# Splitting every fourth feature tile of the up projection by DMAs instead of by ScalarE and VectorE

## The chip, the cores and the metric

The kernel runs on one core of a Trainium2 chip. The time is device microseconds of one execution; the kernel before takes 1145.16 us (median of two runs, 1145.02 and 1145.30). The profile is that of a further execution, whose span, from the first to the last instruction, is 1144.0 us.

## The reference

One layer of a hybrid encoder block on x of shape (1, 256, 2048), all in float32:

```python
proj = x @ w_in                      # 2048 -> 5440, split into retention and latent parts
ret_out = silu(gate) * groupnorm(retention(rope(q), rope(k), v))      # 8 heads of 128
mla_out = latent_attention(c_q, c_kv, k_rope)                          # 8 heads of 128
x = layer_norm(alpha * x + concat(ret_out, mla_out) @ w_out)
h = square(relu(x @ w_up)) @ w_down                                    # 2048 -> 8192 -> 2048
x = layer_norm(alpha * x + h)
```

The change touches `x @ w_up` alone: 2048 by 8192 weights, 64 MB.

## The kernel before

Each large product is made of three cheaper ones. Weights and activations are split into a high part, rounded to the type float32r, and a low part, the rest. High by high, low by high and high by low are summed in PSUM; low by low is left out.

The weights come once from DRAM in the order of their use. A *job* is one load of up to 128 x 2048 floats (1 MB) into one of three raw tiles (`NRAW = 3`), issued on SP's queue (L152). A job is worked off in *pieces* of 1024 columns. For each piece ScalarE casts the raw columns into a high tile (L166) and VectorE subtracts the high tile from the raw one into a low tile (L167). High and low tiles come from a pool with five slots each (`NSLOT = 5`).

The order of the work is that of the program's text; there is no scheduler. After each stretch of matmuls the kernel calls `unit()`, which lets side work advance and then emits further pieces, as many as it is asked for, as long as the piece five before the next one is marked as used (`next_piece`, L113). Whenever a piece of job j is emitted, the loads up to job j + 2 are emitted too.

In the up projection (L864 to L877) one job is one feature tile: 128 output features, 16 blocks of 128 rows of the contraction. A tile `ft` has two pieces of eight blocks. For each block, `wstat` (L582) issues two matmuls: the high weights with 512 columns of activations (both parts of 256 tokens, L584), and the low weights with 256 columns (the high part alone, L585). After each piece its slot is marked free and `unit()` is called, so the end of the first piece of tile ft makes room for the second piece of tile ft + 2, and the end of its second piece makes room for the first piece of tile ft + 3. After a tile's second piece `up_evac` adds the two halves of the PSUM bank (ScalarE's copy, L847, and VectorE's add, L848) and squares the positive part (L849). PSUM has eight banks, taken in turn, so several tiles may wait for their evacuation.

Each engine works its instructions off in the order in which they were emitted; the waits between engines, and those for DMAs, are put in where tiles are shared. GpSimd has the rare powers of minus one half for the norms (L250) and a part of the last norm; between the first layer norm and the second it has nothing to do.

Of the kernel before, what the change touches and what calls it, by code (L numbers as in the profile page):

```python
# [8 lines left out]
F32 = mybir.dt.float32  # L9
# [3 lines left out]
ALU = mybir.AluOpType  # L13
# [23 lines left out]


class Cols:
    """Columns held in pieces of 1024."""  # L40

    def __init__(self, pieces):
        self.pieces = pieces
# [4 lines left out]


class Job:  # L50
    """One load and the pieces of work that it feeds."""

    def __init__(self, load, pieces, slotted):
        self.load = load
# [9 lines left out]
def kernel(  # L64
# [19 lines left out]
    nc = tc.nc  # L84
# [4 lines left out]
    slab = ctx.enter_context(tc.tile_pool(name="slab", bufs=3))  # L89
# [4 lines left out]
    work = work_cm.__enter__()  # L94
    psum = ctx.enter_context(tc.tile_pool(name="psum", bufs=4, space=bass.MemoryType.PSUM))

    def acc(name):
        return psum.tile([P, 512], F32, tag="acc", name=name)
# [1 line left out]
    def bank(name):  # L100
        return psum.tile([P, 512], F32, tag="wk", name=name)

# [1 line left out]
    jobs = []  # L104
    holders = []
    state = {"dma": 0, "job": 0, "unit": 0}
# [31 lines left out]
    def raw_tile(job, name):  # L138
        job.raw = wraw.tile([P, 2048], F32, tag="raw", name=name)
        return job.raw  # L140

    def weights(src, n, name, first=False, into=None):
        job = Job(None, [], into is None)
        cuts = [0, 256, 512, 1024, n]

        def load():
            raw = raw_tile(job, f"raw_{name}")
            if first:
                for a, b in zip(cuts, cuts[1:]):
                    nc.sync.dma_start(raw[:, a:b], src[:, a:b])  # L150
            else:
                nc.sync.dma_start(raw[:, :n], src)  # L152

        def piece(i):
            a, m = i * 1024, min(1024, n - i * 1024)
            if into is None:
                hi = wsp.tile([P, 1024], F32R, tag="hi", name=f"hi_{name}_{i}")
                lo = wsp.tile([P, 1024], F32R, tag="lo", name=f"lo_{name}_{i}")
            else:
                hi, lo = into(i)  # L160
            job.hi.append(hi)
            job.lo.append(lo)
            for o, e in ((0, 256), (256, 512), (512, 1024)) if first and i == 0 else ((0, m),):
                c = slice(o, e)
                r = job.raw[:, a + c.start:a + c.stop]
                nc.scalar.copy(hi[:, c], r)  # L166
                nc.vector.tensor_sub(lo[:, c], r, hi[:, c].bitcast(F32))  # L167

        job.load = load
        job.pieces = [lambda i=i: piece(i) for i in range((n + 1023) // 1024)]  # L170
        job.free = [[False] for _ in job.pieces]
        jobs.append(job)
        return job
# [5 lines left out]
        jobs.append(job)  # L179
        return job  # L180

    # side streams advance one stage for each unit of the main stream of products
    side = []

    def unit(pieces=2):
# [5 lines left out]
            if not next_piece(False):  # L191
                break

# [1 line left out]
    xhl = slab.tile([P, KT, 512], F32R, tag="slab", name="xhl")  # L195

    def x_job(k0, n):
        def load(job):
            nc.sync.dma_start(raw_tile(job, f"xraw{k0}")[:, : n * S], x_t[:, k0 * S:(k0 + n) * S])

        def piece():
            v = job.raw[:, : n * S].rearrange("p (k t) -> p k t", k=n)
            nc.vector.tensor_copy(xhl[:, k0:k0 + n, 0:S], v)
            nc.vector.tensor_sub(xhl[:, k0:k0 + n, S:], v, xhl[:, k0:k0 + n, 0:S].bitcast(F32))

        job = other(load, [piece])

# [1 line left out]
    ident = const.tile([P, P], F32, name="ident")  # L209
    mask = const.tile([P, P], F32, name="mask")  # L210
    invf = const.tile([P, 96], F32, name="invf")
# [38 lines left out]
        nc.gpsimd.tensor_tensor(dst, t[:, :n], mhalf[:, :n], op=ALU.pow)  # L250

    def rot(dst1, dst2, raw, cs, sn, n, w):
        """Rotate n pairs of halves, all first halves ahead of all second ones; raw is used up."""
        c = cs.unsqueeze(1).broadcast_to([P, 2 * n, w])
        s = sn.unsqueeze(1).broadcast_to([P, 2 * n, w])
        v = raw.rearrange("p (a w) -> p a w", w=w)
        t = work.tile([P, 512], F32, tag="t2", name="t2")
        t = t[:, 0:2 * n * w].rearrange("p (a w) -> p a w", w=w)
        nc.vector.tensor_mul(t, v, s)
        nc.vector.tensor_mul(v, v, c)  # L260
        nc.vector.tensor_sub(dst1, v[:, 0:n], t[:, n:2 * n])
        nc.vector.tensor_add(dst2, v[:, n:2 * n], t[:, 0:n])

    def xstat(accs, steps, widths, first, last, tb, banks=None):
        """accs[j] += (h + l)[:, kt, tb].T @ (hi + lo)[:, off + ...] for each
        (hl, kt, hi, lo, off) of steps; l.T @ lo lies below float32's last bit."""
        for i, (hl, kt, hi, lo, off) in enumerate(steps):
            h = hl[:, kt, tb * P:(tb + 1) * P]
            l = hl[:, kt, S + tb * P:S + (tb + 1) * P]
            for x_part, w_part, fst, lst in ((h, hi, True, False), (h, lo, False, False), (l, hi, False, True)):  # L270
                a = off
                for j, w in enumerate(widths):
                    if banks is None or j in banks:
                        nc.tensor.matmul(accs[j][:, :w], x_part, w_part[:, a:a + w],  # L274
                                         start=first and fst and i == 0,
                                         stop=last and lst and i == len(steps) - 1)
                    a += w

# [1 line left out]
    x_job(0, 1)  # L280
    j_mla, j_ret, j_out = [], [], []
    for k in range(KT):
# [34 lines left out]
    for half in range(2):  # L317
        row = []
        for i in range(KT // 2):
            kp = (i + H // 2) % (KT // 2)  # L320
            n = i - (KT // 2 - 3)
            row.append(weights(w_out[half, kp], 2048, f"wo{half}{kp}",
                               into=staged_out(n) if half and n >= 0 else None))
        j_out.append(row)
    j_up = [weights(w_up[ft], 2048, f"wu{ft}") for ft in range(64)]
    j_down = []
    norm_rows = {}

# [16 lines left out]
    row_job(2, [])  # L345
    row_job(3, [])

# [1 line left out]
    nc.gpsimd.memset(warm, 0.0)  # L349
    am = [[acc("m0"), acc("m1"), bank("m2")], [acc("m3"), acc("m4"), bank("m5")]]  # L350
    for i in range(8):
        nc.tensor.matmul(am[1][0][:, 0:P], warm, warm, start=True, stop=True)
    MW = (512, 512, 320)
    # regions of one slab: qnT | knT | v | qrT | krT | kz
    ml = slab.tile([P, 8192], F32, tag="slab", name="ml")
    qnT = ml[:, 0:2048].rearrange("p (h t) -> p h t", h=H)
    knT = ml[:, 2048:4096].rearrange("p (h t) -> p h t", h=H)
    vv = ml[:, 4096:6144].rearrange("p (b c) -> p b c", b=2)
    qrT = ml[:, 6144:7168].rearrange("p (g t) -> p g t", g=4)
    krT = ml[:, 7168:7680].rearrange("p (c t) -> p c t", c=2)  # L360
    lat = ml[:, 2048:2048 + 2 * NMLA].rearrange("p (b c) -> p b c", b=2)
    kz = ml[:, 7680:8192].rearrange("p (b c k) -> p b c k", b=2, c=2)
    nc.gpsimd.memset(kz, 0.0)

    for kt in range(KT):
        hi, lo = use(j_mla[kt])
        last = kt == KT - 1
# [61 lines left out]
    side.append(latent_norm())  # L429
    mix = slab.tile([P, KT, 512], F32R, tag="slab", name="mix")  # L430

# [1 line left out]
    def ret_proj(c, attn):  # L433
        ac = [[acc(f"r{c}_{tb}{j}") for j in range(2)] for tb in range(2)]
        for kp in range(KT // 2):
# [100 lines left out]

    ret_proj(0, ret_attn)

# [1 line left out]
    def q_rope(pq):  # L540
        raw = knT.rearrange("p h t -> p (h t)")[:, 0:1024].rearrange("p (b c) -> p b c", b=2)
        rqo = knT.rearrange("p h t -> p (h t)")[:, 1024:2048].rearrange("p (b h a w) -> p b h a w", b=2, h=8, a=2)
# [17 lines left out]
    for g in range(2):  # L560
        hi, lo = use(j_qr[g])
# [7 lines left out]
    for g in range(2):  # L569
        hi, lo = use(j_uv[g])  # L570
# [17 lines left out]
    for h in range(H):  # L588
        hi, lo = use(j_qk[h])
# [5 lines left out]
        free(j_qk[h])  # L595
        unit()

# [1 line left out]
    att = mid.tile([P, 4, 384], F32, tag="mid", name="att")  # L599

    def mla_attn(h):
# [43 lines left out]
    for c in range(1, 4):  # L645
        ret_proj(c, ret_attn)

# [1 line left out]
    xm = mid.tile([P, 5120], F32, tag="mid", name="xm")  # L649
    xt = xm[:, 0:2 * D].rearrange("p (b c) -> p b c", b=2)  # L650
    spare = xm[:, 2 * D:].rearrange("p (b i c) -> p b i c", b=2, i=4)
# [15 lines left out]
    for half in range(2):  # L667
        ao = [[acc(f"o{half}{tb}{j}") for j in range(2)] for tb in range(2)]
        for i in range(KT // 2 - 3 * half):
            if half == 1 and i == 0:  # L670
                assert not side
                work_cm.__exit__(None, None, None)
                work = ctx.enter_context(tc.tile_pool(name="work2", bufs=1))
            steps = out_steps(half, i)
# [14 lines left out]
        rss[tb] = stat.tile([P, 1], F32, tag="lnrs", name="lnrs")  # L689
        rsqrt_eps(rss[tb], mvs[tb][:, 1:2], 1)  # L690

# [1 line left out]
    w_staged = []  # L693
    for i in range(3):
        w_staged += out_steps(1, KT // 2 - 3 + i)
    x1hl = slab.tile([P, KT, 512], F32R, tag="slab", name="x1hl")
    pts = {}

    # K tiles in order; ks is a range of them
    xf = work.tile([P, 2, 4, P], F32, tag="xf", name="xf")  # L700

    def full(k):
# [32 lines left out]
    first_pb = [acc(f"up{ft}") for ft in range(NSPLIT)]  # L735

    def up_half(tb, ks, fts=range(NSPLIT)):
        """The hi part of the first feature tiles' weights for one block of tokens."""
        t = slice(tb * P, (tb + 1) * P)
        for ft in fts:  # L740
            if ft == len(first_pb):
                first_pb.append(acc(f"up{ft}"))
            hi, lo = use(j_up[ft], (ks[-1] + 8) // 8)
            pb = first_pb[ft].rearrange("p (a t) -> p a t", a=2)
            for k in ks:
                nc.tensor.matmul(pb[:, :, t], hi[:, k * P:(k + 1) * P],  # L746
                                 x1hl[:, k].rearrange("p (a t) -> p a t", a=2)[:, :, t],
                                 start=tb == 0 and k == 0, stop=False)
# [45 lines left out]
    for q in range(3):  # L794
        up_half(0, q4[q])
# [42 lines left out]
    for ft in range(NSPLIT):  # L838
        free(j_up[ft])

# [1 line left out]
    rr = [slab.tile([P, 32, S], F32, tag="slab", name=f"rr{i}") for i in range(2)]  # L842

    def up_evac(ft, pb):
# [19 lines left out]
    for ft in range(NSPLIT, 64):  # L864
        hi, lo = use(j_up[ft])
# [10 lines left out]
                r_split(0)  # L876
            unit()  # L877

# [1 line left out]
    ad = [[(acc if j < 2 else bank)(f"d{tb}{j}") for j in range(4)] for tb in range(2)]  # L880
    for kt in range(60):
        hi, lo = use(j_down[kt])
# [5 lines left out]
        if kt % 4 == 1:  # L888
            r_split(kt // 4 + 1)

# [1 line left out]
    w_staged = []  # L892
    for kt in range(60, 64):
        hi, lo = use(j_down[kt])
# [38 lines left out]
    for j in range(4):  # L933
        down_bank(1, j)
        if j < 2:
            c = (0, j * 512, j * 512 + 512)
# [94 lines left out]
```

## Time and profile before

| | |
|---|---|
| time, median of two runs | 1145.16 us |
| span of the profiled execution | 1144.0 us |
| that execution's time outside the span | taken as the difference to the median, 1.2 us |
| up projection, first to last start of its paired matmuls | 435.9 to 783.2 us |
| TensorE busy, share of the span | 99% |
| VectorE, ScalarE, GpSimd | 60%, 44%, 2% |
| moved by DMA | 217.12 MB, mean 190 GB/s |

Rows of groups read: line, engine, operation, result from operands, shape, count, then busy time in us and the mean of one in ns, then the idle time of the engine just ahead of them and what ended it. Rows of the time order begin with the start and the duration in us; a bracket gives the idle time before and what ended it. Rows of stretches give the stretch, its length, the busy time of TensorE, its weight loads, VectorE, ScalarE and GpSimd with the number of instructions, then the granted TensorE clock (1.00 is full), the busy share of the 16 DMA engines and the GB/s that they moved. Rows of DMA issues end with KB each and the median us from issue to landing. Rows of one tile's instructions give minimum, median and maximum duration in ns and the first and last start.

### The profile page before, as it was taken

How to read it: one execution, taken by the hardware profiler on the slowest of the kernel's cores; microseconds unless marked ns; L12 is line 12 of the kernel's file. 1: busy time of each engine (PE TensorE's matmuls, PEld its weight loads, DVE VectorE, ACT ScalarE, POOL GpSimd, SP SyncE). 2: the span in 40 equal slices, each digit the busy share in tenths (PEclk: the TensorE clock that was granted, in tenths of full speed). 3: DMA queues.
4: the chain of work that ended last, by engine and by line, in shares of the span. 5: the costliest groups of instructions: out<-in, count | busy, mean ns of one | idle time of the engine just before them, and what ended most of it. 6: DMA issues, size and time to landing. Idle time of an engine off the chain costs nothing.

```text
span 1144.0 us, 14163 instructions
## 1 busy us (share of the span) xinstructions
PE 1127.5 (99%) x5636; PEld 952.7 (83%) x5636; DVE 687.6 (60%) x919; ACT 506.7 (44%) x653; POOL 18.2 (2%) x23
## 2 busy tenths in 40 slices
PE   8999999999999999999999999999999999999995
PEld 7888888888888889888888888888888888888884
DVE  5776674666656786555555655555656455445567
ACT  4445664545453545444444444444434444344340
POOL 0000000000000000000000000000000000000003
PEclk9999999999999999999999999999999999999998
DMA  7765364444474625555555555555566555555561
GB/s 227 254 210 208 116 222 178 157 148 160 152 294 177 236 103 196 190 188 190 189 188 185 185 184 184 184 185 184 187 223 237 199 184 189 203 197 184 189 252 74
DMA packets 34049, 217.12 MB, mean 190 GB/s; under 512 B 4160, under 2 KB 5312, under 8 KB 10560
## 3 DMA queue, kind: packets, MB, share of 16 engines
q1 hardware_dynamic: 33552, 215.44, 53.2%
q8 instruction: 44, 0.72, 0.2%
q10 hardware_dynamic: 432, 0.79, 0.2%
q14 instruction: 21, 0.17, 0.0%
HBM read 214.12 MB, written 2.10 MB: 189 GB/s over the span
## 4 chain that ended last, share of the span: by engine, by line
PE 95%; DVE 2%; DMA 1%; POOL 1%; ACT 1%; issue 0%; SPq 0%; ACTq 0%; DVEq 0%; POOLq 0%
PE d L274 29%; PE up L584 20%; PE r L274 15%; PE up L585 10%; PE o L274 7%; PE m L274 4%; PE pu L584 2%; DMA raw_mla<-in_w_mla 1%; PE pv L274 1%; PE pu L585 1%; PE pq L274 1%; PE up L746 1%; PE pms L608 0%; PE pms L607 0%; PE up L754 0%
## 5 line engine op out<-in xcount | busy, mean ns | idle before, releaser
L584 PE MATMUL up<-x1hl,hi_wu 128*128 128x512 f32 x984 | 347.7, 399 | 0.0
L585 PE MATMUL up<-x1hl,lo_wu 128*128 128x256 f32 x984 | 276.4, 281 | 0.0
L274 PE MATMUL d<-hi_wd,rhl 128*128 128x512 f32 x992 | 248.4, 389 | 0.0
L167 DVE TENSOR_TENSOR lo_wd<-raw_wd,hi_wd 128x1024 fp32r<-128x1024 f32 x124 | 146.6, 1221 | 158.3 <-ACT hi_wd L166 158.1
L584 PEld LDWEIGHTS up<-x1hl,hi_wu 128*128 128x128 f32 x984 | 184.9, 188 | 46.0
L274 PEld LDWEIGHTS d<-hi_wd,rhl 128*128 128x128 f32 x992 | 186.2, 188 | 38.6
L166 ACT CAST hi_wd<-raw_wd 128x1024 fp32r<-128x1024 f32 x124 | 125.1, 1053 | 191.3 <-PE d L274 182.8
L167 DVE TENSOR_TENSOR lo_wu<-raw_wu,hi_wu 128x1024 fp32r<-128x1024 f32 x128 | 156.4, 1225 | 74.1 <-ACT hi_wu L166 70.0
L585 PEld LDWEIGHTS up<-x1hl,lo_wu 128*128 128x128 f32 x984 | 185.9, 189 | 0.0
L166 ACT CAST hi_wu<-raw_wu 128x1024 fp32r<-128x1024 f32 x128 | 134.1, 1051 | 83.0 <-PE up L584 80.7
L274 PE MATMUL r<-hi_ret,xhl 128*128 128x512 f32 x512 | 147.1, 397 | 0.0
L274 PE MATMUL d<-lo_wd,rhl 128*128 128x512 f32 x496 | 134.5, 389 | 0.0
L274 PEld LDWEIGHTS d<-lo_wd,rhl 128*128 128x128 f32 x496 | 93.1, 188 | 19.3
L274 PEld LDWEIGHTS r<-hi_ret,xhl 128*128 128x128 f32 x512 | 93.9, 188 | 18.3
L167 DVE TENSOR_TENSOR lo_ret<-raw_ret,hi_ret 128x1024 fp32r<-128x1024 f32 x64 | 75.7, 1220 | 23.0 <-ACT hi_ret L166 22.9
L274 PE MATMUL r<-lo_ret,xhl 128*128 128x512 f32 x256 | 79.4, 391 | 0.0
L847 ACT COPY ut<-up 128x256 f32<-128x256 f32 x64 | 23.9, 373 | 118.9 <-PE up L585 116.2
L166 ACT CAST hi_ret<-raw_ret 128x1024 fp32r<-128x1024 f32 x64 | 64.9, 1051 | 14.5 <-PE r L274 11.6
L848 DVE TENSOR_TENSOR ut<-ut,up 128x256 f32<-128x256 f32 x64 | 27.0, 421 | 65.3 <-ACT ut L847 65.3
L274 PE MATMUL o<-hi_wo,mix 128*128 128x512 f32 x208 | 57.1, 392 | 0.0
L274 PEld LDWEIGHTS r<-lo_ret,xhl 128*128 128x128 f32 x256 | 48.0, 188 | 10.4
L274 PE MATMUL m<-hi_mla,xhl 128*128 128x512 f32 (+1 forms) x192 | 46.1, 372 | 0.9 <-ACT hi_mla L166 0.8
(182 smaller groups left out, 980.7 us busy)
## 6 DMA issues: line engine op xcount, KB each, us to landing
raw_wu<-in_w_up SPq DMA_DIRECT2D x64, 1024.0 KB, 4.8
raw_wd<-in_w_down SPq DMA_DIRECT2D x64, 1024.0 KB, 4.8
raw_ret<-in_w_ret SPq DMA_DIRECT2D x32, 1024.0 KB, 4.8
raw_wo<-in_w_out SPq DMA_DIRECT2D x16, 1024.0 KB, 4.8
raw_mla<-in_w_mla SPq DMA_DIRECT2D x15, 672.0 KB, 5.5
raw_qk<-in_w_qk SPq DMA_DIRECT2D x8, 640.0 KB, 3.9
row<-in_ln_rows SPq DMA_DIRECT2D x4, 1024.0 KB, 4.8
raw_uv<-in_w_uv SPq DMA_DIRECT2D x2, 1024.0 KB, 4.7
```

The lines of the kernel that those rows point to most:

```text
L166: nc.scalar.copy(hi[:, c], r)
L167: nc.vector.tensor_sub(lo[:, c], r, hi[:, c].bitcast(F32))
L274: nc.tensor.matmul(accs[j][:, :w], x_part, w_part[:, a:a + w], start=first and fst and i == 0, stop=last and lst and i == len(steps) - 1)
L584: nc.tensor.matmul(pb, hi[:, a:a + P], hl[:, k0 + i], start=first and i == ks[0], stop=False)
L585: nc.tensor.matmul(pb[:, 0:S], lo[:, a:a + P], hl[:, k0 + i, 0:S], start=False, stop=last and i == ks[-1])
L746: nc.tensor.matmul(pb[:, :, t], hi[:, k * P:(k + 1) * P], x1hl[:, k].rearrange("p (a t) -> p a t", a=2)[:, :, t], start=tb == 0 and k == 0 ...
L847: nc.scalar.copy(t, pb[:, S:])
L848: nc.vector.tensor_add(t, t, pb[:, 0:S])
```

## The change

For the feature tiles 9, 13, 17, ... 61 (14 of 64, 28 of 128 pieces) nothing is loaded into a raw tile. Instead, for each piece: GpSimd issues a DMA that reads the 128 x 1024 floats from DRAM and writes the high tile, of type float32r, converting on the way; ScalarE writes the negated high tile into the low tile; GpSimd issues a second DMA of the same floats that adds them to the low tile. The low part is thus raw minus high, as before. The other 50 tiles are split as before. The parameter `dma_lo` is added too, and no call sets it.

```diff
-    def weights(src, n, name, first=False, into=None):
+    def weights(src, n, name, first=False, into=None, dma_lo=False, dma_hi=False):
         job = Job(None, [], into is None)
         cuts = [0, 256, 512, 1024, n]
 
         def load():
+            if dma_hi:
+                return
             raw = raw_tile(job, f"raw_{name}")
...
             job.hi.append(hi)
             job.lo.append(lo)
+            if dma_hi:
+                nc.gpsimd.dma_start(hi[:, :m], src[:, a:a + m])
+                nc.scalar.mul(lo[:, :m], hi[:, :m].bitcast(F32), -1.0)
+                nc.gpsimd.dma_start(lo[:, :m], src[:, a:a + m], accum_op=ALU.add)
+                return
             for o, e in ((0, 256), (256, 512), (512, 1024)) if first and i == 0 else ((0, m),):
                 c = slice(o, e)
                 r = job.raw[:, a + c.start:a + c.stop]
                 nc.scalar.copy(hi[:, c], r)
-                nc.vector.tensor_sub(lo[:, c], r, hi[:, c].bitcast(F32))
+                if dma_lo:
+                    nc.scalar.mul(lo[:, c], r, -1.0)
+                    nc.gpsimd.dma_start(lo[:, c], src[:, a + o:a + e], accum_op=ALU.add)
+                else:
+                    nc.vector.tensor_sub(lo[:, c], r, hi[:, c].bitcast(F32))
...
-    j_up = [weights(w_up[ft], 2048, f"wu{ft}") for ft in range(64)]
+    j_up = [weights(w_up[ft], 2048, f"wu{ft}", dma_hi=ft % 4 == 1 and ft > 8) for ft in range(64)]
```

In the changed kernel the lines of the split move down: the converting DMA is L166, the negation L167, the accumulating DMA L168, the cast L173, the subtract L178, the pair of matmuls L595 and L596, the evacuation's copy L858.

## The prediction

> **What bounds the kernel now.** I read the page first (busy shares, the chain that ended last, the costliest groups), then the stretches of 100 us, then the time order of ScalarE inside the up projection.
>
> ```profile
> span 1144.0 us, 14163 instructions
> PE 1127.5 (99%) x5636; PEld 952.7 (83%) x5636; DVE 687.6 (60%) x919; ACT 506.7 (44%) x653; POOL 18.2 (2%) x23
> PE 95%; DVE 2%; DMA 1%; POOL 1%; ACT 1%; issue 0%; SPq 0%; ACTq 0%; DVEq 0%; POOLq 0%
> L584 PE MATMUL up<-x1hl,hi_wu 128*128 128x512 f32 x984 | 347.7, 399 | 0.0
> L585 PE MATMUL up<-x1hl,lo_wu 128*128 128x256 f32 x984 | 276.4, 281 | 0.0
> 600.00:700.00 100.00, 100.00 (x567) 86.76 (x567) 59.05 (x72) 43.27 (x55) 0.00 (x0) 1.00 0.52 183
> ```
>
> TensorE carries 95% of the chain. In the up projection it is busy for 100.00 of 100 us at granted clock 1.00, and its two groups have 0.0 us of idle time before them: no split, load or evacuation is late. VectorE (59 of 100 us), ScalarE (43) and the DMA engines (share 0.52) all wait for TensorE. So the change takes work from engines that don't set the end. It can gain nothing unless matmuls themselves get quicker, and it loses as soon as its own chain is longer than the lead that the slots give. That lead is the number to find.
>
> ```profile
> L584 PE MATMUL up<-x1hl,hi_wu x984: 395/398/403, 435.9 to 783.2; 128*128 128x512 f32 x197
> 599.89 1.05 ACT L166 CAST hi_wu<-raw_wu 128x1024 fp32r<-128x1024 f32 x1 [1.39 <-PE up L584]
> 602.83 0.37 ACT L847 COPY ut<-up 128x256 f32<-128x256 f32 x1 [1.89 <-PE up L585]
> 603.10 1.05 ACT L166 CAST hi_wu<-raw_wu 128x1024 fp32r<-128x1024 f32 x1
> 605.54 1.05 ACT L166 CAST hi_wu<-raw_wu 128x1024 fp32r<-128x1024 f32 x1 [1.40 <-PE up L584]
> 604.18 1.23 DVE L167 TENSOR_TENSOR lo_wu<-raw_wu,hi_wu 128x1024 fp32r<-128x1024 f32 x1
> 602.22 22.95 SPq L152 DMA_DIRECT2D raw_wu<-in_w_up  x5
> ```
>
> The 984 pairs (one matmul by high weights, one by low) start from 435.9 to 783.2 us, so a pair takes 347.3 / 983 = 0.353 us. A piece of 1024 columns is eight pairs, 2.83 us, and a feature tile 5.65 us, which is also the distance of the casts at 599.89 and 605.54. There are five slots: a piece may be made when the piece five before it has been used, and is needed four pieces later, 4 x 2.83 = 11.3 us after its slot came free. Call t0 the moment when the slot of a tile's first piece comes free: the first piece is due at t0 + 11.3, the second, whose slot comes free 2.83 us later, at t0 + 14.1. Today a piece needs a cast (1.05) and a subtract (1.23), some 2.5 us with what stands ahead of it, so almost 9 us of lead lie unused.
>
> **What is removed.** For 14 tiles (9, 13, ... 61), 28 pieces: 28 x 1.23 = 34 us of VectorE; 28 casts, replaced by 28 negations of the same shape (taken as 1.05 us each, so ScalarE's sum stays); 14 loads of 1 MB on SP's queue. All of it lies under TensorE, as the zero idle time shows: worth 0 us.
>
> **What is added and where it stands.** On GpSimd's queue, empty in this stretch (0.00 busy, x0, in the row above), now stand four DMAs for each such tile. First that queue in the changed program, with its waits (tile 9, then the first piece of 13):
>
> ```order
> L166 DMA hi_wu_0_3884<-in_w_up 128x1024 [waits DVE_49,PE_49]
> L168 DMA lo_wu_0_3885<-in_w_up 128x1024 [waits PE_49,Activation_49]
> L166 DMA hi_wu_1_3906<-in_w_up 128x1024 [waits DVE_49,PE_49]
> L168 DMA lo_wu_1_3907<-in_w_up 128x1024 [waits Activation_49]
> L166 DMA hi_wu_0_4072<-in_w_up 128x1024 [waits DVE_49,PE_49]
> ```
>
> The second DMA waits for ScalarE's negation, which waits for the first DMA to land. The third, the high part of the second piece, is queued behind that wait although its slot is free at t0 + 2.83. So the two pieces of a tile run one after the other, not side by side.
>
> ScalarE's queue before, at the same place (tile 9 is made from raw_wu_3790):
>
> ```order
> L847 COPY ut<-up_3843 128x256
> L166 CAST hi_wu_0_3886<-raw_wu_3790 128x1024
> L166 CAST hi_wu_1_3907<-raw_wu_3790 128x1024
> L847 COPY ut<-up_3890 128x256
> L166 CAST hi_wu_0_3933<-raw_wu_3837 128x1024
> ```
>
> And now:
>
> ```order
> L858 COPY ut<-up_3841 128x256
> L167 ACTIVATE lo_wu_0_3885<-hi_wu_0_3884 128x1024
> L167 ACTIVATE lo_wu_1_3907<-hi_wu_1_3906 128x1024
> L858 COPY ut<-up_3889 128x256
> L173 CAST hi_wu_0_3933<-raw_wu_3835 128x1024
> ```
>
> Nothing changed place, but two casts that found their data in SBUF became two negations that wait for DMAs just issued. Behind them on ScalarE stand the evacuation of tile 7 and the casts of tile 10, and behind those VectorE's subtract.
>
> **The price of one DMA.** No converting, accumulating or GpSimd-issued DMA is in this trace. The nearest rows are these:
>
> ```profile
> raw_wu<-in_w_up SPq DMA_DIRECT2D x64, 1024.0 KB, 4.8
> raw_qk<-in_w_qk SPq DMA_DIRECT2D x8, 640.0 KB, 3.9
> L152 SPq DMA_DIRECT2D raw_wu<-in_w_up x64: 327/328/328, 392.3 to 754.9; - x64
> L250 POOL TENSOR_TENSOR rstd<-rs,mhalf 128x4 f32<-128x4 f32 x4 | 4.1, 1035 | 264.2 <-DVE rs L249 264.2
> ```
>
> - 512 KB: from 640 KB (3.9 us) to 1024 KB (4.8) is 0.9 us for 384 KB, so 512 KB of data cost 1.2 us and a plain DMA of that size lands in 3.9 - 0.3 = 3.6 us.
> - Issue: 0.33 us on SP. On GpSimd it may be the same (0.33), or 1.03 us like its smallest routine arithmetic, or more. I take 1.0, by the row of the same engine: 0.7 more per DMA.
> - Conversion: 0 extra at the low end; at the high end as much again as the data (1.2). I take 0.
> - Accumulation: it reads the source and also the tile. From 0 extra to several times the data; I take one more pass, 1.2 us.
>
> The Trainium skill (DMA: Bandwidth & Descriptors, section "Anatomy of one DMA") prices a GpSimd-issued DMA at about 2.0 us plus bytes by 436 GB/s, an estimate of 3.2 us here; no run here shows it, and it speaks for the second rival below.
>
> **The chain for one tile**, from t0:
> 1. High part of piece 0: 3.6 + 0.7, and 1.2 because an SP load of 1 MB starts beside it (SP's issue at 602.22, the slot's release just ahead of the copy at 602.83): 5.5.
> 2. Negation: 1.05 and 0.2 for two hops: 6.75.
> 3. Issue of the first accumulation, ahead of the next DMA on GpSimd: 1.0, so 7.75.
> 4. High part of piece 1: 4.3, and 1.2 behind the first accumulation's data: 13.25.
> 5. Negation: 14.5.
> 6. Second accumulation: 4.3 + 1.2: 20.0.
>
> Due at 14.1: TensorE waits 5.9 us per tile. The first accumulation lands at 6.75 + 5.5 = 12.25, due at 11.3, and so is part of that wait. Next behind: tile 10's first piece. ScalarE is free at 14.5, copies (0.37), casts (1.05), VectorE subtracts (1.23): 17.2 us, due at 17.0 + 5.9, so it adds nothing. The wait is not won back, since t0 of the next such tile hangs on TensorE's own progress: 14 x 5.9 = 83 us.
>
> **A second cost, the clock.**
>
> ```profile
> 1131.00:1132.00 1.00, 0.89 (x4) 0.39 (x3) 0.19 (x2) 0.00 (x0) 0.98 (x1) 1.00 0.35 131
> 1134.00:1135.00 1.00, 0.00 (x0) 0.00 (x0) 0.52 (x2) 0.32 (x1) 0.45 (x1) 1.00 0.00 0
> 1135.00:1136.00 1.00, 0.00 (x0) 0.00 (x0) 1.00 (x3) 0.49 (x1) 0.43 (x1) 0.55 0.00 0
> 0.99 3.78 PE L352 MATMUL m<-warm 128*128 128x128 f32 x16 [0.99 <-POOL warm L349]
> 4.97 0.64 PE L274 MATMUL m<-hi_mla,xhl 128*128 128x512 f32 x1 [0.20 <-ACT hi_mla L166]
> 6.82 0.92 PE L274 MATMUL m<-lo_mla,xhl 128*128 128x512 f32 x3
> ```
>
> After the last matmul (about 1131.9) the granted clock falls to half at about 1135.1, 3.2 us later. A wait of 5.9 us in one or two parts can reach that. What the way back costs is bounded by the start: the 512-column matmul at 4.97 still took 0.64 us where the mean is 0.40, those at 6.82 run close to full pace, so slow running lasts at most from 0.99 to 6.8, a loss of some 2.6 us at half pace, and at least 0. I take the middle, 1.3: 14 x 1.3 = 18 us. The Trainium skill (TensorE: Matmul & The Clock Gate, "The HAM clock gate") puts both the fall and the recovery at a window of about 3.4 us; the fall agrees with the 3.2 us read here. By its recovery, 3.4 us at half pace, the term would be an estimate of 14 x 1.7 = 24 us.
>
> Sum against the profiled execution: 1144.0 + 83 + 18 = 1245; its span lies 1.2 us under the median of 1145.16, which gives 1246 us.
>
> **The rivals.**
> - *The chain fits.* GpSimd's DMAs land like SP's, the accumulation costs no second pass, and the parallel load takes nothing: 3.6 + 1.25 + 0.33 + 3.6 + 1.25 + 3.6 = 13.6, due at 14.1. TensorE never waits: 1145 us. For it: the DMA engines are only half used, and the page's price of 3.2 us gives it more room. Against it: three landings in a row leave 0.5 us, and any single surcharge above uses that up. The point of decision is 0.17 us each; to stay within 2% the chain may reach 14.1 + 23/14 = 15.7 us. This ends on the other side, not slower.
> - *The accumulation is dear.* Read, add and write may run far below copying pace. With 6 us per pass instead of 1.2, steps 4 and 6 grow by 4.8 each: 15.5 + 1.3 per tile, 14 x 16.8 = 235, some 1380 us. For it: no row here shows a DMA that computes. Against: no row shows one as slow either.
> - *A gain.* Less VectorE and ScalarE traffic would have to shorten the pair of 0.353 us. Against it: matmuls stand back to back with the other engines idle half the time. That the conversion doesn't round, and the low part becomes zero, would change values and not the time: the matmuls are the same.
>
> **How the numbers follow.** The chain overruns by 1.6 to 14.7 us per tile, 1168 (no clock loss) to 1370 (with 1.3 each): 0.64, likeliest 1246. It fits or nearly: 0.17, at 1145 to 1168. Dearer than that: 0.18. A gain above 2%: 0.01. About 2% (23 us) is what a measurement of this kernel tells from no change: slower 0.82, same 0.17, faster 0.01. The range takes in the second case from 1144 and ends at 1370, leaving 0.18 and 0.01 outside.
>
> **What would show it.** In the profile after: idle time before the low-weight group of the up projection, released by the accumulating DMA, in about 14 places of some 6 us, near none elsewhere; the landing time of the two kinds of GpSimd DMA in the list of issues (4.3 and 5.5 by my sum); GpSimd's issue near 1 us; ScalarE's negations waiting 5 us or more for the high part; granted clock under 1.00 in the up projection. The prediction is wrong if TensorE keeps 100 of 100 us there, if the first piece rather than the second is late, or if the accumulation takes over 8 us.

## The result and the profile after

The changed kernel takes 1264.89 us (median of two runs, 1263.57 to 1266.21) against 1145.16 us: 1.105 times as long, with an interval of 1.102 to 1.108. Its profiled execution has a span of 1264.4 us, 120.4 us more than the 1144.0 us of before.

The page of the changed kernel, in the same order as before: busy shares, TensorE's granted clock in 40 slices, the chain that ended last, the costliest group with the weight loads that belong to it, and the two new kinds of DMA.

```profile
span 1264.4 us, 14212 instructions
PE 1157.9 (92%) x5636; PEld 973.1 (77%) x5636; DVE 648.2 (51%) x891; ACT 502.1 (40%) x653; POOL 58.3 (5%) x79
PEclk9999999999999999988899999888899999999998
PE 61%; issue 23%; DMA 9%; DVE 3%; ACT 2%; POOL 1%; SPq 0%; ACTq 0%; POOLq 0%; DVEq 0%
L596 PE MATMUL up<-x1hl,lo_wu 128*128 128x256 f32 x984 | 291.4, 296 | 89.8 <-DMA lo_wu<-in_w_up 89.8
L596 PEld LDWEIGHTS up<-x1hl,lo_wu 128*128 128x128 f32 x984 | 198.9, 202 | 98.7 <-DMA lo_wu<-in_w_up 98.7
hi_wu<-in_w_up POOLq DMA_DIRECT2D x28, 512.0 KB, 6.0
lo_wu<-in_w_up POOLq DMA_DIRECT2D x28, 512.0 KB, 5.5
```

TensorE's share falls from 99% to 92%. The low-weight matmuls, with 0.0 us idle before them in the kernel before, now have 89.8 us, and their weight loads, which feel the wait first, 98.7 us, all of it ended by the accumulating DMA. The granted clock, which was 0.9 or more in every slice but the last before, now falls into the eights in two stretches of the middle. ("Issue", 23% of the chain, is time for which the profile shows no wait.)

The time from the first to the last pair of the up projection tells that the loss lies there, and the waits by releaser tell in how many places. First the row of the pairs of the changed kernel:

```profile
L595 PE MATMUL up<-x1hl,hi_wu x984: 387/395/633, 435.7 to 903.4; 128*128 128x512 f32 x197
```

From 435.7 to 903.4 it is 467.7 us, where it was 347.3: 120.4 us more, as much as the span grew. And the waits:

```profile
POOL hi_wu L166 <- PE up L596: 236.4, 14, 40.2
ACT lo_wu L167 <- DMA hi_wu<-in_w_up: 176.8, 28, 8.0
PEld up L596 <- DMA lo_wu<-in_w_up: 98.7, 28, 6.3
```

TensorE waits 28 times, for each of the 28 pieces, 98.7 / 14 = 7.05 us for a tile. What is left, 120.4 - 98.7 = 21.7 us, 1.55 for a tile, I put down to matmuls at a lower clock. The order of time bears it out: besides the 28 waits, 85 of the 983 distances between the starts of pairs are stretched (over 0.42 us, most of them 0.64, where 0.353 was usual), 23 us in all. One tile in order of time, with GpSimd's issues, ScalarE's negations and TensorE's two waits:

```profile
555.55 0.56 POOL L166 DMA_DIRECT2D hi_wu<-in_w_up  x1 [16.03 <-PE up L596]
562.25 0.87 POOL L168 DMA_DIRECT2D lo_wu<-in_w_up  x1 [6.14 <-ACT lo_wu L167]
562.81 0.87 POOL L166 DMA_DIRECT2D hi_wu<-in_w_up  x1
570.94 0.86 POOL L168 DMA_DIRECT2D lo_wu<-in_w_up  x1 [7.26 <-ACT ut L858]
560.89 1.06 ACT L167 ACTIVATE lo_wu<-hi_wu 128x1024 fp32r<-128x1024 f32 x1 [5.11 <-DMA hi_wu<-in_w_up]
569.58 1.06 ACT L167 ACTIVATE lo_wu<-hi_wu 128x1024 fp32r<-128x1024 f32 x1 [7.63 <-DMA hi_wu<-in_w_up]
567.84 0.39 PE L596 MATMUL up<-x1hl,lo_wu 128*128 128x256 f32 x1 [1.15 <-DMA lo_wu<-in_w_up]
576.52 0.58 PE L596 MATMUL up<-x1hl,lo_wu 128*128 128x256 f32 x1 [5.63 <-DMA lo_wu<-in_w_up]
```

The slot comes free at about 555.4. High DMA to negation 5.34 us, negation to the first accumulation's issue 1.36, the next high DMA 0.56 behind it, 6.77 to its negation, 1.36 to the second accumulation, 5.58 until TensorE goes on: 21.0 us from the first issue. (Over the 14 tiles the medians of the two high DMAs, from issue to negation, are 5.4 and 6.4 us; this tile's second one is among the longer.) The second piece was due 14.1 us after the slot. (The bracket of the last accumulation names ScalarE's copy, which ran last ahead of it; by the program it waits for the negation, done at 570.64.)

The stretches behind the second wait show the clock:

```profile
572.00:574.00 2.00, 0.00 (x0) 0.00 (x0) 2.00 (x2) 2.00 (x4) 0.00 (x0) 1.00 0.77 92
574.00:576.00 2.00, 0.00 (x0) 0.00 (x0) 1.97 (x4) 0.95 (x2) 0.00 (x0) 0.57 1.00 215
578.00:580.00 2.00, 2.00 (x8) 1.71 (x7) 0.00 (x0) 0.00 (x0) 0.00 (x0) 0.50 0.86 283
580.00:582.00 2.00, 2.00 (x11) 1.74 (x10) 0.13 (x1) 0.54 (x2) 0.00 (x0) 0.73 0.75 311
```

TensorE stops at 570.9; the granted clock falls to half at about 574.3 and is back at about 581.1, some 4.6 us after the matmuls began again.

### The profile page after: what moved, and what is told of

Same layout as the page of the kernel before. It is cut to its first block, busy times and chain, and to the rows that moved or that the text cites. A ratio compares the mean times of both kernels' runs of the same rounds, so it can differ in the third digit from the quotient of the medians.

```text
span 1264.4 us, 14212 instructions
## 1 busy us (share of the span) xinstructions
PE 1157.9 (92%) x5636; PEld 973.1 (77%) x5636; DVE 648.2 (51%) x891; ACT 502.1 (40%) x653; POOL 58.3 (5%) x79
## 3 DMA queue, kind: packets, MB, share of 16 engines
q0 software_dynamic: 8064, 29.36, 10.2%
## 4 chain that ended last, share of the span: by engine, by line
PE 61%; issue 23%; DMA 9%; DVE 3%; ACT 2%; POOL 1%; SPq 0%; ACTq 0%; POOLq 0%; DVEq 0%
PE d L285 28%; PE r L285 14%; DMA hi_wu<-in_w_up 5%; PE o L285 5%; PE m L285 4%; PE up L595 2%; DMA lo_wu<-in_w_up 2%; PE pu L595 1%; DVE lo_wu L178 1%; PE up L596 1%; ACT hi_wu L173 1%; PE pv L285 1%; DMA raw_mla<-in_w_mla 1%; PE pu L596 1%; PE pq L285 1%
## 5 line engine op out<-in xcount | busy, mean ns | idle before, releaser
L596 PE MATMUL up<-x1hl,lo_wu 128*128 128x256 f32 x984 | 291.4, 296 | 89.8 <-DMA lo_wu<-in_w_up 89.8
L595 PE MATMUL up<-x1hl,hi_wu 128*128 128x512 f32 x984 | 369.3, 416 | 0.0
L596 PEld LDWEIGHTS up<-x1hl,lo_wu 128*128 128x128 f32 x984 | 198.9, 202 | 98.7 <-DMA lo_wu<-in_w_up 98.7
L595 PEld LDWEIGHTS up<-x1hl,hi_wu 128*128 128x128 f32 x984 | 197.4, 201 | 47.2
L178 DVE TENSOR_TENSOR lo_wd<-raw_wd,hi_wd 128x1024 fp32r<-128x1024 f32 x124 | 146.6, 1222 | 158.3 <-ACT hi_wd L173 158.1
L173 ACT CAST hi_wd<-raw_wd 128x1024 fp32r<-128x1024 f32 x124 | 125.1, 1053 | 191.4 <-PE d L285 182.4
L178 DVE TENSOR_TENSOR lo_wu<-raw_wu,hi_wu 128x1024 fp32r<-128x1024 f32 x100 | 119.5, 1222 | 25.3 <-ACT hi_wu L173 23.4
L173 ACT CAST hi_wu<-raw_wu 128x1024 fp32r<-128x1024 f32 x100 | 101.6, 1050 | 29.7 <-PE up L595 24.4
L167 ACT ACTIVATE lo_wu<-hi_wu 128x1024 fp32r<-128x1024 f32 x28 | 29.7, 1061 | 176.8 <-DMA hi_wu<-in_w_up 176.8
L178 DVE TENSOR_TENSOR lo_ret<-raw_ret,hi_ret 128x1024 fp32r<-128x1024 f32 x64 | 75.7, 1220 | 23.0 <-ACT hi_ret L173 22.9
L858 ACT COPY ut<-up 128x256 f32<-128x256 f32 x64 | 23.6, 369 | 123.2 <-PE up L596 120.5
L173 ACT CAST hi_ret<-raw_ret 128x1024 fp32r<-128x1024 f32 x64 | 64.9, 1050 | 14.5 <-PE r L285 11.7
```

Source lines behind the costliest of these rows:

```text
L167: nc.scalar.mul(lo[:, :m], hi[:, :m].bitcast(F32), -1.0)
L595: nc.tensor.matmul(pb, hi[:, a:a + P], hl[:, k0 + i], start=first and i == ks[0], stop=False)
L596: nc.tensor.matmul(pb[:, 0:S], lo[:, a:a + P], hl[:, k0 + i, 0:S], start=False, stop=last and i == ks[-1])
L858: nc.scalar.copy(t, pb[:, S:])
```

## The experiments

The theory: nothing but TensorE's wait counts; it comes from the chain of one tile being longer than the lead of its slots, above all because GpSimd's queue puts the two pieces one after the other, and each long wait adds a stretch at half clock. The rivals: the 56 DMAs have a price of their own (traffic, the cost of adding), or ScalarE, blocked behind the landings, makes the other tiles late. Each ratio is against the kernel before, timed beside it (medians of 1145.03 to 1145.25 us); what a run gives back of the 120 us is counted from the changed kernel's 1264.89 us above.

**The low part alone by DMA.** The high part is cast from a raw tile again.

```diff
-    j_up = [weights(w_up[ft], 2048, f"wu{ft}", dma_hi=ft % 4 == 1 and ft > 8) for ft in range(64)]
+    j_up = [weights(w_up[ft], 2048, f"wu{ft}", dma_lo=ft % 4 == 1 and ft > 8) for ft in range(64)]
```

> The same 14 tiles, but only the low part by DMA: SP loads the raw tile as before, ScalarE casts the high part and writes the negated raw tile into the low tile, GpSimd's accumulating DMA adds the DRAM data (here it is left open that low becomes raw minus raw, so the low part of these tiles is zero). The lead theory: the chain of a piece is a cast of 1.05, a negation of 1.06, a hop of 0.3 and an accumulation of 5.5, some 8 us from its slot, under the 11.3 us of lead, and no piece waits on GpSimd for another: TensorE never waits, 1145 us. Rival, the accumulating DMAs themselves disturb TensorE or the loads: 28 of the 56 GpSimd DMAs are left, so about half of the loss stays, some 1205 us.

Measured: 1148.68 us, 1.003 times the kernel before (1.002 to 1.004). The waits of TensorE in this run:

```profile
PEld up L596 <- DMA lo_wu<-in_w_up: 6.8, 13, 1.7
```

With the landing of the high DMA out of the chain, the wait all but goes, though 28 accumulating DMAs are still issued. I had expected no wait at all; the accumulations land in 7.3 us here (median; 10.6 at most), where the changed kernel had 5.5. All 64 of SP's loads are back in this run, but whether they lengthen the landings was not tested.

**The second high DMA ahead of the first accumulation.** One order on GpSimd's queue is altered.

```diff
                 nc.gpsimd.dma_start(hi[:, :m], src[:, a:a + m])
+                if i == 1:
+                    nc.gpsimd.dma_start(job.lo[0], src[:, 0:1024], accum_op=ALU.add)
                 nc.scalar.mul(lo[:, :m], hi[:, :m].bitcast(F32), -1.0)
-                nc.gpsimd.dma_start(lo[:, :m], src[:, a:a + m], accum_op=ALU.add)
+                if i == 1:
+                    nc.gpsimd.dma_start(lo[:, :m], src[:, a:a + m], accum_op=ALU.add)
```

> The changed kernel with one order altered: GpSimd issues the high DMA of the second piece ahead of the accumulation of the first. Nothing else changes. The lead theory: high 1 is issued when its slot comes free, at t0 + 2.8, lands at about t0 + 8.8, is negated by 9.9, its accumulation is issued at 10.2 and lands at 15.7, due at 14.1: 1.6 us per tile instead of 7.05, too short for the clock to fall, so 1145 + 22 = 1167 us. Rival, the loss comes from the traffic and the price of the DMAs and not from their order: landings stretch when they overlap, the wait stays near 7 us, 1250 us or more. Second rival, ScalarE's blocked queue: it is blocked for as long as before by the first landing, so at least half of the loss would stay, 1205 us.

Measured: 1161.83 us, 1.015 (1.013 to 1.016). The waits, the pairs and a stretch of this run:

```profile
PEld up L599 <- DMA lo_wu<-in_w_up: 20.2, 15, 1.9
L598 PE MATMUL up<-x1hl,hi_wu x984: 389/391/403, 434.8 to 797.8; 128*128 128x512 f32 x197
600.00:700.00 100.00, 95.96 (x549) 83.56 (x548) 45.72 (x61) 40.02 (x51) 12.09 (x17) 1.00 0.73 223
```

The same DMAs and the same bytes, and 103 of 120 us are gone: 20.2 us of waiting are left, 1.4 us for a tile against the 1.6 expected, and the clock stays at 1.00. Neither traffic nor ScalarE's queue can have been more than a small part.

The run is only 16.7 us longer than the kernel before, less than its 20.2 us of waiting, because the matmuls got a little quicker: the median high-weight matmul takes 391 ns where it took 398. In order of time the pairs stand 0.346 us apart in long stretches, which begin mostly at a wait, and 0.353 us apart in the others; the kernel before has 0.353 throughout. That is 3.7 us in this run and 2 us in the changed kernel. What sets the pace, the runs don't show.

**One piece in each of 28 tiles.** As many DMAs, no two pieces of one tile.

```diff
-    j_up = [weights(w_up[ft], 2048, f"wu{ft}", dma_hi=ft % 4 == 1 and ft > 8) for ft in range(64)]
+    j_up = [weights(w_up[ft], 2048, f"wu{ft}", dma_hi=ft % 2 == 1 and ft > 8) for ft in range(64)]
...
-            if dma_hi:
-                return
...
-                nc.sync.dma_start(raw[:, :n], src)
+                w = 1024 if dma_hi else n
+                nc.sync.dma_start(raw[:, :w], src[:, :w])
...
-            if dma_hi:
+            if dma_hi and i == 1:
```

> As many converting and accumulating DMAs as in the changed kernel (28 of each), but spread: only the second piece of each of the 28 odd tiles 9, 11, ... 63 is made by DMA, the first piece by a load of half the tile, a cast and a subtract as before. The lead theory: each chain stands alone on GpSimd, 5.3 + 1.06 + 0.3 + 5.5 = 12.2 us with hops, due at 11.3: 0.9 us each, 28 x 0.9 = 26, no fall of the clock, 1171 us. Rival, the price is per DMA (traffic, disturbance of TensorE): the same 56 DMAs cost the same 120 us, 1265 us.

Measured: 1196.74 us, 1.043 (1.038 to 1.047). More than half of the loss goes, but 26 us more than expected stay. The list of issues and the waits of this run:

```profile
hi_wu<-in_w_up POOLq DMA_DIRECT2D x28, 512.0 KB, 6.9
lo_wu<-in_w_up POOLq DMA_DIRECT2D x28, 512.0 KB, 5.4
PEld up L595 <- DMA lo_wu<-in_w_up: 41.6, 17, 4.2
```

I had put 5.3 us for the high landing, the shortest in the changed kernel; here its median is 6.9. I had also expected no fall of the clock; it falls here too, to 0.96 in the mean from 600 to 700 us. Whether SP's loads do that was tried next.

**The same with SP's loads cut**, and **the changed kernel with SP's loads cut.** From tile 13 on, SP loads 256 columns instead of 2048 (or 1024) of the other tiles, and cast and subtract read these four times.

```diff
-                nc.sync.dma_start(raw[:, :n], src)
+                w = 256 if few else n
+                nc.sync.dma_start(raw[:, :w], src[:, :w])
...
-                r = job.raw[:, a + c.start:a + c.stop]
+                r = job.raw[:, 0:256].unsqueeze(1).broadcast_to([P, 4, 256]) if few else job.raw[:, a + c.start:a + c.stop]
```

> The kernel with one piece in each of the 28 odd tiles made by DMA (measured at 1197 us where 1171 were expected, with a median high landing of 6.9 us), and the same cut of SP's loads to 256 columns from tile 13 on. If the loads beside it explain the missed 26 us: the high landing falls to about 4.1, the chain to 4.1 + 1.06 + 0.3 + 5.5 = 11.0 us with hops near 11.3, and the time to 1150 us. If the landing is long for a reason of GpSimd's own: 6.9 stays and the time stays near 1197 us.

Measured: 1157.07 us, 1.011 (1.010 to 1.013). The high landing of this run:

```profile
hi_wu<-in_w_up POOLq DMA_DIRECT2D x28, 512.0 KB, 4.4
PEld up L597 <- DMA lo_wu<-in_w_up: 13.0, 15, 2.6
```

From 6.9 to 4.4 us: with chains this close to their due time, SP's loads decide, and they explain what had been missed in the run before.

> The changed kernel in which SP loads, from tile 13 on, only 256 of the 2048 columns of the tiles that are split as before (cast and subtract read these columns again and again, so their cost stays; the weights of these tiles are then not the right ones). It takes the SP loads from beside the GpSimd DMAs. The prediction put 1.2 us into the first high landing for that load: it falls from 5.3 to about 4.1, the wait from 7.05 to 5.9 us, 13 x 1.2 = 16 us less, 1249 us. If the loads weigh nothing: 1265 us. If they are the main cause of the long landings: the wait falls under 3 us and the clock term with it, 1190 us or less.

Measured: 1259.04 us, 1.100 (1.098 to 1.101). In the changed kernel itself the loads weigh little: TensorE waits 88.6 us instead of 98.7, 0.8 us less for each of 13 tiles where 1.2 were expected. Only 6 us of time come of it, as more of the pairs run at the lower clock (0.958 in the mean of the profiled execution, 0.969 in the changed kernel's).

```profile
PEld up L599 <- DMA lo_wu<-in_w_up: 88.6, 28, 6.3
```

**Writing instead of adding.** The second DMA loses `accum_op=ALU.add`; its waits stay.

> The changed kernel with the second DMA of each piece writing instead of adding, with the same waits; the low part then holds the raw weights. It measures what adding costs. If it reads the tile as one more pass, as the prediction took, 1.2 us each: the low landing falls from 5.5 to 4.3, the high DMA behind it lands 1.2 earlier, the wait falls from 7.05 to 4.6 us per tile, 14 x 2.4 = 34 us less, 1231 us. If adding costs nothing beside copying: 1265 us. If adding is the main cost of the low DMA: its landing falls to the SP row's 3.6 us or under, the wait to 3 us, 1200 us or less.

Measured: 1223.80 us, 1.069 (1.067 to 1.070). The list of issues and the software queue of this run; for the queue, in the changed kernel, the page has 10.2% with the same packets and bytes.

```profile
q0 software_dynamic: 8064, 29.36, 7.6%
hi_wu<-in_w_up POOLq DMA_DIRECT2D x28, 512.0 KB, 5.2
lo_wu<-in_w_up POOLq DMA_DIRECT2D x28, 512.0 KB, 4.1
PEld up L596 <- DMA lo_wu<-in_w_up: 57.2, 21, 4.1
```

Adding costs 5.5 - 4.1 = 1.4 us of a landing. The queue's engine time says the same: 10.2% of 1264.4 us less 7.6% of 1223.2 us is 36 us, 1.3 us for each of 28 accumulations. The high DMA of the second piece, which stands behind the accumulation, reaches its negation in 5.0 to 5.3 us, where it took 6.2 to 7.2; that of the first piece keeps its 5.4 us in the median. So an accumulation costs about as much as one more pass of 512 KB (1.2 us in the prediction) and is not a dear operation; it makes a third of the loss because its price stands in the chain twice.

**TensorE kept busy while it waits.** 22 spare matmuls ahead of the second piece of each such tile.

```diff
+            if ft % 4 == 1 and ft > 8 and p == 1:
+                fb = bank(f"fill{ft}")
+                for q in range(NFILL):
+                    nc.tensor.matmul(fb, x1hl[:, q % KT, 0:P], x1hl[:, q % KT], start=True, stop=True)
```

> The changed kernel with 22 spare matmuls of 512 columns (22 x 0.216 = 4.8 us) on activations already there, into a bank that nobody reads, ahead of the second piece of each of the 14 tiles, where TensorE waits nearly 6 us anyway. The clock theory: of the 120 us lost, 14 x 7.05 = 99 are waiting and 22 are matmuls at half clock after a wait; with TensorE kept busy the granted clock stays at 1.00 and the 22 us go, 1243 us. Rival, the matmuls are slow there because of the DMAs that write SBUF beside them: the 22 us stay, 1265 us. Second rival, the spare matmuls don't fit the wait: 1265 us or more.

Measured: 1248.08 us, 1.090 (1.088 to 1.091), faster than the changed kernel by 17 us in the medians and 20.5 us in the profiled spans, with 308 matmuls more. The waits, and a stretch:

```profile
PEld up L597 <- DMA lo_wu<-in_w_up: 34.2, 27, 2.6
600.00:700.00 100.00, 95.02 (x513) 80.56 (x512) 36.92 (x49) 30.16 (x41) 8.52 (x12) 1.00 0.60 181
```

The granted clock stays at 1.00 in this stretch (0.93 in the same stretch of the changed kernel). A group of 22 spare matmuls takes 5.0 us of TensorE (from the first at 565.60 to the next pair at 570.65, for one), 70 us in 14 tiles. Waiting and spare work together, 34.2 + 70 = 104 us, cover the 99.9 us by which this span exceeds that of before: the wait is about as long as ever, and the slow matmuls are all but gone. So the clock term is shown, and DMAs that write beside the matmuls are not what slows them.

**Buffers of their own for eight tiles.** Tiles 9 to 37 take two buffers that are free until tile 40.

```diff
+    def into_big(i):
+        t = work.tile([P, 2048], F32R, tag="big", name=f"wub{i}", bufs=2)
+        return t[:, 0:1024], t[:, 1024:2048]
...
-    j_up = [weights(w_up[ft], 2048, f"wu{ft}", dma_hi=ft % 4 == 1 and ft > 8) for ft in range(64)]
+    j_up = [weights(w_up[ft], 2048, f"wu{ft}", dma_hi=ft % 4 == 1 and ft > 8,
+                into=into_big if ft % 4 == 1 and 8 < ft < 40 else None) for ft in range(64)]
```

> The changed kernel, but the pieces of the 8 tiles 9, 13, ... 37 get two buffers of their own (which lie idle until tile 40) instead of slots. Their high DMA may go as soon as the tile four before has been used, some 20 us ahead instead of 11.3. The lead theory: the chain of 20.9 us then ends in time for these tiles; the other six still cost 7.05 + 1.55 each: 1145 + 6 x 8.6 = 1197 us, with TensorE at 100 of 100 us before tile 40. Rival, the traffic or the price of the DMAs: no difference in their number, 1265 us.

Measured: 1209.59 us, 1.056 (1.055 to 1.058). TensorE's waits, for the six tiles with slots and the eight without:

```profile
PEld up L601 <- DMA lo_wu<-in_w_up: 42.3, 12, 6.1
PEld up L601 <- DMA wub<-in_w_up: 14.7, 8, 2.1
```

The six cost 42.3 / 6 = 7.05 us each, as before; the eight 1.8 us each instead of nothing. Lead removes most of the wait, but not all of it, as I had expected: TensorE is busy for 57.3 of 60 us from 560 to 620. In this run the DMAs of the eight land in 7.5 us (median), and what lengthened them there was not separated; with the order altered as well (next run) these tiles wait for nothing.

**Both cures together.**

> Both cures at once: the second piece's high DMA ahead of the first accumulation, and own buffers for the 8 tiles up to 37. All 56 GpSimd DMAs are still there. The lead theory: the eight tiles wait for nothing, the other six some 1.45 us each as in the reordered kernel, 1145 + 9 = 1154 us. If the traffic of the GpSimd DMAs has a price of its own that no order takes away: above 1162 us, the time of the reordered kernel.

Measured: 1152.30 us, 1.006 (1.005 to 1.008), with 8.1 us of waiting, all of it in the tiles with slots:

```profile
PEld up L604 <- DMA lo_wu<-in_w_up: 8.1, 7, 1.6
```

All 56 DMAs are there and 113 of 120 us are gone. No version beats the kernel before: it keeps TensorE busy for 100 of 100 us there, and the change removes work from other engines alone. What a version could still gain is the pace of the pairs, 983 x 0.007 = 7 us by an estimate from the two distances above if the shorter one held throughout; no run got there.

## Why the prediction was right, point by point

- *What bounds the kernel, and what the removed work is worth*: right. No run without the 28 casts, 28 subtracts and 14 loads is faster than the kernel before.
- *The two pieces of a tile run one after the other on GpSimd*: right, and the main cause; taking it away alone gives back 103 of 120 us. (More lead or a cheaper second DMA also gives much back, since the chain only has to get under its due time; the shares of the causes don't add up.)
- *The wait per tile*: 7.05 us, forecast 5.9. The term that was mis-sized is step 4, the high DMA behind the accumulation: 5.5 forecast, 6.77 measured in the tile shown and 6.4 in the median. Without adding it is 5.0, so the accumulation's data ahead of it on the same queue is what it waits for. Step 1 came out right in sum (5.34 for 5.5) by luck: with SP's loads cut it is 4.7 in the median, so the DMA alone was put too low (4.3) and the load beside it, 0.7 us, too high (1.2). GpSimd's issue keeps its queue for 0.56 us ahead of the next DMA, not 1.0; hop, negation and hop take 1.36 rather than 1.25. Steps 2, 3, 5 and 6 so nearly cancel (2 x 1.36 + 0.56 + 5.58 = 8.9 for 9.0), which is luck too.
- *The places*: 14 of some 6 us were forecast. The waits are 28, since the first piece is late too, by about 1.4 us; the chain had that in its 12.25 against 11.3, the list of signs did not.
- *One accumulation costs one more pass, 1.2 us*: right, 1.3 to 1.4. That conversion costs nothing extra fits the 4.1 us of the second DMA without adding, which also writes float32r, under my 4.3, but an unconverted one from GpSimd was not run.
- *The clock*: right in kind, 1.55 us per tile for 1.3. The prediction's bound from the start is a little low: half of the 5.8 us from 0.99 to 6.8 is 2.9 rather than 2.6, and the middle, 1.45, would have been nearer. The fall came some 3.4 us after the last matmul, the way back took 4.6 us in the tile shown. The Trainium skill (TensorE: Matmul & The Clock Gate, "The HAM clock gate") has one window of about 3.4 us or more for both; this tile agrees, with 3.4 and 4.6 us. A wait doesn't have to last that long, as the last section shows.
- *Tile 10 is not late in turn*: right; all 98.7 us of the weight loads' wait are put down to the accumulating DMA.
- *The rival in which the chain fits*: it would have needed three landings of 3.6 us. Measured are 4.1 to 4.4 for an undisturbed high DMA or a low one without adding, and 5.4 with adding. The Trainium skill (DMA: Bandwidth & Descriptors, "Anatomy of one DMA"), by which I had estimated 3.2 us, is below every one of these. (The prediction says that this price speaks for the second rival; it speaks for this one, the first.) The rival of a dear accumulation fell with the same numbers.
- *The rival of a gain*: right that no run gained. But back-to-back matmuls, its reason, don't fix the pair at 0.353 us: pairs 0.346 us apart, 2% less, occur in long stretches of the runs above.
- The forecast of 1246 us was 19 us low: 14 x 1.15 = 16 for the wait and 14 x 0.25 = 3.5 for the clock.

## What to carry to other kernels

Before work is moved from an idle engine to a chain of DMAs, count the chain from the moment its buffer comes free to the moment it is due, landing by landing, and compare it with the lead that the buffers give: here 21.0 us against 14.1, on engines of which none but TensorE was busy for more than 60% of the time. On GpSimd's queue, which works in order, a DMA that waits for another engine holds back everything behind it: issue all the DMAs that can go at once ahead of the first that must wait (1265 to 1162 us here, by one order). And where TensorE waits, add the stretch at half clock that can follow: it followed every wait of over 5 us in the changed kernel, and in other runs some waits of 2 to 3 us and not others.

## What the runs showed of the hardware

- An accumulating DMA keeps the DMA engines busy for longer than a copy of as many bytes. By the busy share of GpSimd's queue above, 56 DMAs without adding take 7.6% of 1223.2 us, 1.7 us of all 16 engines each; if the high ones take the same in the changed kernel, 10.2% of 1264.4 us leaves 2.9 us for one accumulation. In the changed kernel, first with the converting high DMA and a load in flight, then with the first accumulation and the high DMA behind it:

```profile
558.00:560.00 2.00, 2.00 (x14) 1.75 (x13) 0.00 (x0) 0.00 (x0) 0.00 (x0) 1.00 1.02 403
564.00:566.00 2.00, 2.00 (x14) 1.75 (x13) 0.00 (x0) 0.00 (x0) 0.00 (x0) 1.00 0.95 147
```

  The 16 engines are all but fully busy in both, with 403 GB/s in the one and 147 in the other.
- A high DMA beside a load can hang on a remainder. With one piece per tile, one issued at 582.84, just behind an SP load of 582.48, was answered by the negation at 590.15:

```profile
587.00:588.00 1.00, 1.00 (x7) 0.89 (x6) 0.00 (x0) 0.00 (x0) 0.00 (x0) 1.00 0.93 332
588.00:589.00 1.00, 1.00 (x7) 0.88 (x6) 0.00 (x0) 0.00 (x0) 0.00 (x0) 1.00 0.08 29
589.00:590.00 1.00, 1.00 (x8) 0.86 (x7) 0.00 (x0) 0.00 (x0) 0.00 (x0) 1.00 0.04 12
```

  For the last 2 us about one engine's worth (0.08 x 16 = 1.3, 0.04 x 16 = 0.6) is busy. Which engine, and why it lags, no run here shows. The Trainium skill (DMA: Bandwidth & Descriptors, "Latency and other measured facts") calls two of the engines usually slower, with a guess that ties it to GpSimd-issued DMAs.
- The length of a wait alone doesn't tell whether the clock falls. In the run with buffers of their own for eight tiles, TensorE was idle for 1.79 us and ran at half clock soon after; with one piece per tile it was idle for 2.96 us and kept the full clock (1.00 in every stretch of 2 us from 710 to 722 as well):

```profile
548.98 0.39 PE L601 MATMUL up<-x1hl,wub 128*128 128x256 f32 x1 [1.79 <-DMA wub<-in_w_up]
550.00:552.00 2.00, 2.00 (x8) 1.72 (x8) 1.56 (x2) 0.00 (x0) 0.00 (x0) 0.50 1.12 414
716.02 0.39 PE L595 MATMUL up<-x1hl,lo_wu 128*128 128x256 f32 x1 [2.96 <-DMA lo_wu<-in_w_up]
718.00:720.00 2.00, 2.00 (x14) 1.75 (x13) 0.00 (x0) 0.00 (x0) 0.00 (x0) 1.00 0.83 311
```

  What decides between them, the runs don't show. That the reordered kernel, with waits of up to 1.9 us, kept its clock at 1.00 is therefore not assured by their shortness.
